# A hybrid SSD and linear-attention layer on one core: the linear-attention state in two buffers, the first sums of A beside the last scan, and w2 loaded in the first unit

## The chip, the cores and the metric

The kernel runs on one core of a Trainium2 chip. A core has a TensorE (PE: matmuls, with a part that loads weights, PEld), a VectorE (DVE), a ScalarE (ACT), a GpSimd (POOL) and a SyncE (SP, which here only issues DMAs). Each engine takes its own instructions in order, and they wait for one another by semaphores. Matmul results land in PSUM, eight banks of 512 float32 for each of 128 partitions; everything else lies in SBUF.

The metric is the device time of one execution in microseconds. A profiled execution also has a span, from its first to its last instruction.

## The reference

One layer on 2048 tokens of width 1024 with 16 meta tokens ahead of them. One input projection feeds two branches, each is projected back, weighed by sigmoid gates and merged:

```python
u = rmsnorm(hres, norm_w)
proj = jnp.einsum('bld,dn->bln', u, w_in)
z, xbc, dt_raw, q, k, v, g_gla, a_lr, merge_g = split_cols(proj, IN_WIDTHS)
...
y_r, _ = ssd_chunked(xs[:, m:], dt[:, m:], a, bm[:, m:], cm[:, m:], SSD_CHUNK, s_m)
...
o_r, _ = gla_chunked(q[:, m:], k[:, m:], v[:, m:], log_a[:, m:], GLA_CHUNK, st_m)
...
branches = jnp.stack([y_ssd.astype(y_gla.dtype), y_gla], axis=2)
branch_proj = jnp.einsum('blnc,ncd->blnd', branches, w_branch)
gates = jax.nn.sigmoid(merge_g.reshape(b, l, N_BRANCH, D_MODEL))
merged = jnp.sum(gates * branch_proj, axis=2)
return hres + jnp.einsum('bld,de->ble', merged, w_out)
```

The final RMSNorm follows, and the meta tokens are dropped. Linear attention (GLA) carries a state from chunk to chunk, for each head 128 by 256:

```python
def step(s, inp):
    qi, ki, vi, gi = inp
    o_inter = jnp.einsum('bhtk,bhkv->bhtv', qi * jnp.exp(gi), s)
    ...
    s_new = jnp.exp(g_last)[..., None] * s + jnp.einsum('bhsk,bhsv->bhkv', k_dec, vi)
    return s_new, o_inter + o_intra
```

## The kernel before

**Two halves.** The first half walks over four blocks of 512 tokens (`b`), and in each over eight units: four groups of SSD heads (`ssd_proj`, L450), then four heads of linear attention (`gla_proj`, L604). A unit projects what its heads need. It yields after each piece of projection (six times), and at each yield the loop at L830 calls `step()`, which lets every generator that has begun run on to its own next yield. So the scan of one unit (`ssd_scan` L494, `gla_scan` L639) runs beside the projection of the next ones. `gates(o)` (L414) and `dt_chain` run in the same way. The second half (from L870) is a list of products of 128 by 128 by 512 blocks: for each stage (merge gates, the two branch projections, twice, then the output projection) seven products of a Strassen-Winograd scheme for each pair of row blocks. A product needs operand tiles of B (`load_b`, `prep_b`) and of A (`load_a`, `sum_a`, `prep_a`); every one is split into a high and a low part, and three matmuls make one exact product (`accum`, L183).

**What sets the order.** On PE and SP the order is the one in which the code issues, written out by hand (`manual_schedule`). On ACT, DVE and POOL a planner places the instructions by its own estimate of times; it may bring a later one forward when its inputs are ready. A tile comes from a pool under a tag with a number of buffers; a new tile of the tag waits until one of them is free. In the second half SP too keeps its written order, and `todo` says after which product an operand is loaded, summed and split: B 12 products ahead, A's loads 9 ahead (`LOAD`), A's splits five ahead (`AHEAD`).

**w2.** `late_constants` (L332) issues four DMAs on SP: three into a staging tile for the gate weights w2, of the tag "acc" (two buffers, used by the convolution of `ssd_proj`), and one for the masks into a "tok4" tile. It is called ahead of unit 1 of block 0 (L835). Weights of the projections pass over the same SP queue (`load_w` L157, `load_raw` L173; three raw buffers), are split by ACT (L165) and POOL (L166), and are written back for the later blocks (L181).

**The meta tokens.** In block 0 `ssd_scan` first makes the state of the 16 meta tokens (`meta_state`, L515: a matmul on PE and a copy on DVE, L519), in the same step as the first chunk's matmul on that state (L565).

**The linear-attention state.** `gla_scan` ends with four chunks, two to a step (L783 to L795). The matmuls of a chunk go into the two halves of one PSUM bank `po`: kd·v into columns 256 to 511, att·v and then q·state into columns 0 to 255. Then DVE updates the state in place (L789) and ACT reads columns 0 to 255 (L791, L793).

**From the first half to the second.** When the last unit's projection is done, the scans of the last heads still run. The dictionary `between` (L1094) gives what is put ahead of each of their remaining steps `k`: the loads of B and A for products 1 and 2 of pairs 0 and 1 of the first stage, their splits and these four products. Pools opened at L860 to L862 lie where the inputs and weights lay; those opened at L1114 and L1115 lie where the scans' tiles lay, so their tiles wait for the scans. The sums of A (`sum_a`, L902, four POOL operations) of pairs 0 and 1 are made in the first `run(-1)` (L1118), from the pool `spl` of the second kind; B's raw tiles, and the snapshots of two early products (L930), come from `rpl`, of the first kind, with five buffers.

Of the kernel before, what the change touches and what calls it, by code (L numbers as in the profile page):

```python
# [20 lines left out]
SG = 4  # L21
# [19 lines left out]
def trunk_kernel(ctx: ExitStack, tc: tile.TileContext, xm, xmt, w_feat, w_tok, w_zm, w_br, w_o,  # L41
# [7 lines left out]
    def mk(pool, shape, dt, tag, **kw):  # L49
        cnt[0] += 1  # L50
        return pool.tile(shape, dt, tag=tag, name=f"{tag}_{cnt[0]}", **kw)
# [278 lines left out]
    msk = const.tile([P, NMSK, P], U8, name="msk")  # L330

    def late_constants():  # L332
        w2r = mk(wk, [P, META + BLK], F32, "acc")[:48, :512]
        for i in range(3):
            nc.sync.dma_start(w2r[16 * i:16 * i + 16, :], gw2)
        nc.scalar.activation(w2, w2r, AF.Copy)
        nc.vector.tensor_tensor(w2[32:48], w2r[32:48], w2[32:48].bitcast(F32), op=ALU.subtract)
        mstg = mk(wk, [P, D], F32, "tok4", bufs=NT4)[:, :NMSK * P]
        nc.sync.dma_start(mstg, cmsk)
        nc.vector.tensor_copy(msk.rearrange("p l t -> p (l t)"), mstg)  # L340
# [153 lines left out]
    def ssd_scan(o, g, feats, zs):  # L494
# [87 lines left out]
        yield  # L582
        if m0:
            meta_state()
        for c in range(1, NCH):
            before(c)
            after(c - 1)
            yield
# [50 lines left out]
    def gla_scan(o, h, qs, kf, vt, vm, gs):  # L639
# [140 lines left out]

        ot = mk(wk, [P, NCH, 256], F32, "ot", bufs=1)
        ssq = mk(sm, [P, 4], F32, "ssq")
        for c in range(NCH):  # L783
            po = bank(pc, "pc")
            vc = [t[:, c] for t in vt]
            accum(po[:, 256:], [t[:, c] for t in kdt], vc, True, True)
            accum(po[:, :256], [t[:, c] for t in atp], vc, True, False)
            nc.tensor.matmul(po[:, :256], qg[:, c * P:(c + 1) * P], s_gla[:, h], start=False, stop=True)
            nc.vector.scalar_tensor_tensor(s_gla[:, h], s_gla[:, h], egl[:, c:c + 1], po[:, 256:],  # L789
                                           op0=ALU.mult, op1=ALU.add)  # L790
            nc.scalar.activation(ot[:, c], po[:, :256], AF.Copy)  # L791
            jk = mk(wk, [P, 256], BF16, "junk", bufs=1)
            nc.scalar.activation(jk, po[:, :256], AF.Square, accum_out=ssq[:, c:c + 1])  # L793
            if c % 2:
                yield  # L795
# [34 lines left out]
    for b in range(nblk):  # L830
        o = new_block(b, next_u[b])
        for i in range(SG + GH):
            if (b, i) in beside:
                begin(beside_unit(beside[b, i]))
            if (b, i) == (0, 1):  # L835
                late_constants()
            if i == 1:
                begin(gates(o))
            if i == SG and b + 1 < nblk:
                begin(fetch_u(b + 1))  # L840
            for _ in ssd_proj(o, i) if i < SG else gla_proj(o, i - SG):
                step()
        save(0)


# [13 lines left out]

    bpl = {p: pool2(f"bops{p}", 4) for p in (1, 2)}  # L860
    rpl = pool2("raws", 1)
    apl = pool2("aops", 7)  # L862
    

    g_left = [[left(f"g_{b}_{i}") for i in range(16)] for b in range(nblk)]
# [4 lines left out]
    class Stage:  # L870
# [8 lines left out]
        def load_b(self, p, j):  # L879
            src = {1: lambda j: self.braw(j, 0), 2: lambda j: self.braw(4 + j, 0), 3: lambda j: self.braw(4 + j, 1),  # L880
                   4: lambda j: self.sums[1][j][:, 1], 5: lambda j: self.sums[0][j][:, 1],
                   6: lambda j: self.sums[1][j][:, 0], 7: lambda j: self.sums[0][j][:, 0]}[p]
            raw = self.braws[p, j] = mk(rpl, [P, BLK], F32, "br", bufs=5)
            nc.sync.dma_start(raw, src(j))

        def prep_b(self, p, j):
# [14 lines left out]

        def sum_a(self, n):  # L902
            a11, a21, a22, a12 = self.araws.pop(n)
            s1, s2, s4 = [mk(spl, [P, 4, P], F32, "as", bufs=6) for _ in range(3)]
            nc.gpsimd.tensor_tensor(s1, a21, a22, op=ALU.add)  # L905
            nc.gpsimd.tensor_tensor(s2, s1, a11, op=ALU.subtract)
            nc.gpsimd.tensor_tensor(a21, a11, a21, op=ALU.subtract)
            nc.gpsimd.tensor_tensor(s4, a12, s2, op=ALU.subtract)
            self.a[n].update({3: s4, 4: a22, 5: s1, 6: s2, 7: a21})
# [8 lines left out]
        def product(self, n, p, early=False):  # L918
            key, pool, tag = {1: ("a", pj, "pj"), 6: ("a",) * 3, 5: ("a",) * 3, 3: ("a",) * 3, 2: ("c", pc, "pc"),
                              7: ("b", pt, "pt"), 4: ("b",) * 3}[p]  # L920
            if p in (1, 2, 7):
                self.ps[n, key] = bank(pool, tag)
            ps = self.ps[n, key]
            a = self.a[n][p]
            for j in range(4):
                bt = self.b[p, j]
                accum(ps, (a[:, 0, j], a[:, 1, j]), (bt[:, 0], bt[:, 1]), p in (1, 2, 7) and j == 0, j == 3,
                      skip_group_check=True)
            if p in (1, 6, 5):
                sn = mk(rpl, [P, BLK], F32, "br", bufs=5) if early else mk(opl, [P, BLK], F32, "sn", bufs=6)  # L930
                nc.scalar.activation(sn, ps, AF.Copy)  # L931
                self.snap[n, p] = sn
            if p in DONE:
                key, sn = {2: ("c", 1), 5: ("b", 5), 4: ("b", 6), 3: ("a", None)}[p]
                self.use(n, *DONE[p], self.ps[n, key], self.snap.get((n, sn)))
# [57 lines left out]
    def out_stage():  # L993
        fns, res, ssq = [], {}, {}

        def fetch(n, i, t):
            r0 = (2 * n + i) * P
            r = res[n, i, t] = io()
            nc.sync.dma_start(r, xm[META + r0:META + r0 + P, t * BLK:(t + 1) * BLK])
            if t and len(fns) < 2:  # L1000
                for hf in range(2):
                    fns.append(mk(rpl, [P, BLK], F32, "br", bufs=5))
                    nc.sync.dma_start(fns[hf], fnw[:, hf * BLK:(hf + 1) * BLK].to_broadcast([P, BLK]))

        def use(n, i, t, ps, snap):
            r0 = (2 * n + i) * P
            r = res[n, i, t]
            x = total(ps, snap)
            nc.vector.scalar_tensor_tensor(r, x, 0.5, r, op0=ALU.mult, op1=ALU.add)
            first = (n, i) not in ssq  # L1010
            if first:
                ssq[n, i] = mk(spl, [P, 2], F32, "ssf")
            q = ssq[n, i]
            jk = mk(spl, [P, BLK], BF16, "junk", bufs=1)
            nc.scalar.activation(jk, r, AF.Square, accum_out=q[:, t:t + 1])
            if not first:
                nc.vector.tensor_tensor(q[:, 0:1], q[:, 0:1], q[:, 1:2], op=ALU.add)
                nc.vector.tensor_scalar(q[:, 0:1], q[:, 0:1], 1.0 / D, EPS, op0=ALU.mult, op1=ALU.add)
                nc.gpsimd.tensor_tensor(q[:, 0:1], q[:, 0:1], mhalf[:, 0:1], op=ALU.pow)
                for hf in range(2):  # L1020
                    o = res[n, i, hf]
                    nc.vector.scalar_tensor_tensor(o, o, q[:, 0:1], fns[hf], op0=ALU.mult, op1=ALU.mult)
                    store(out[r0:r0 + P, hf * BLK:(hf + 1) * BLK], o)

        return Stage("out", ("o",), seq // (2 * P),
                     lambda n, i, j: m_left[(2 * n + i) // 4][j][:, :, (2 * n + i) % 4 * P:((2 * n + i) % 4 + 1) * P],
                     fetch, use)
# [27 lines left out]
        st.sum_a(n)  # L1055

    for i, (st, n, p) in enumerate(order):
        if p == 1:
            at(i - LOAD + (n % 2), lambda st=st, n=n, i=i: st.sum_a(n) if i < NEARLY else load_sum_a(st, n))
    for si, st in enumerate(stages):  # L1060
        for q in range(0 if si else 8, 28):
            p, j = PS[q // 4], q % 4
# [25 lines left out]
    def flush(due):  # L1088
# [2 lines left out]


    st = stages[0]
    between = {  # L1094
        0: [lambda: [st.load_b(1, j) for j in range(4)], lambda: st.load_a(0)],
        1: [lambda: [st.prep_b(1, j) for j in range(4)], lambda: st.prep_a(0, 1)],
        2: [lambda: [st.load_b(2, j) for j in range(4)], lambda: st.load_a(1)],
        3: [lambda: st.product(0, 1, True), lambda: [st.prep_b(2, j) for j in range(4)], lambda: st.prep_a(0, 2)],
        4: [lambda: st.prep_a(1, 1)],
        5: [lambda: st.product(0, 2), lambda: st.prep_a(1, 2)],  # L1100
        6: [lambda: flush(stores[:]), lambda: stores.clear(), lambda: st.product(1, 1, True)],
        7: [lambda: st.product(1, 2)],
        8: [lambda: flush(stores[:]), lambda: stores.clear()],
    }
    k = 0
    while running or begun or k in between:
# [6 lines left out]
    first.close()  # L1113
    bpl.update({p: pool2(f"bops{p}", 4, side="right") for p in (6, 7, 5, 3, 4)})  # L1114
    opl, spl = pool2("outs", 1, side="right"), pool2("small", 4, side="right")  # L1115

    with tc.manual_schedule(engines={mybir.EngineType.SP}):
        run(-1)  # L1118
# [94 lines left out]
```

## Time and profile before

| | us |
|---|---|
| median of 3 runs | 2356.83 |
| lowest and highest | 2351.35, 2357.54 |
| the profiled execution's own time | 2356.45 |
| its span | 2354.7 |
| mean granted clock of TensorE | 0.985 |

| engine | busy us | share of the span |
|---|---|---|
| PE | 2252.8 | 96% |
| DVE | 1553.0 | 66% |
| ACT | 1183.3 | 50% |
| POOL | 679.4 | 29% |

The first half takes about 1560 us of the span, the second the rest. In lines of the timeline the first number is the start in microseconds from the span's beginning, the second the duration; then follow engine, source line, operation, tile written and tiles read, shape, and in brackets how long the engine was idle before it and who ended that. `SPq` and `ACTq` are DMA issues on those queues; `x4` means four instructions in a row. In lines of waits stand the total, the count and the longest one. A busy PE isn't PE at its peak: after an idle stretch the granted clock can fall to half for some microseconds.

### The profile page before, as it was taken

The page shows a single profiled execution, that of the slowest core. Times are in us where ns is not written, and L with a number is a line of the kernel's source. Part 1 is how long each engine was busy: PE and PEld are TensorE (multiplying, and loading weights), DVE is VectorE, ACT ScalarE, POOL GpSimd, SP SyncE. Part 2 cuts the span into 40 slices and gives each one's busy share as a digit, 9 for nine tenths or more (in the row PEclk, how much of TensorE's full clock was granted, in tenths as well). Part 3 has the DMA queues.
Part 4 walks back from the last instruction along what each step waited for, and adds up shares of the span by engine and source line. Part 5 has one row for each costly group of instructions (what it writes and reads, how often), then busy time and mean ns, then how long its engine had stood idle before and what let it go on. Part 6 is the DMA issues. An engine that isn't in the chain of part 4 may idle for free.

```text
span 2354.7 us, 36479 instructions
## 1 busy us (share of the span) xinstructions
PE 2252.8 (96%) x12641; PEld 1956.3 (83%) x12641; DVE 1553.0 (66%) x2895; ACT 1183.3 (50%) x2758; POOL 679.4 (29%) x681
## 2 busy tenths in 40 slices
PE   7799999999999999999999999879999999999998
PEld 7689889889888988888988898758888878878786
DVE  5577665666576667566568655664578864778875
ACT  4565655455534455543456443554554444554543
POOL 3334433122311212221122200037423254413341
PEclk9899999999999999999999999989999999999999
DMA  7665875666886666787676655547577866777753
GB/s 270 216 209 180 301 243 186 207 218 212 265 269 201 209 220 215 241 259 225 194 227 217 206 169 161 171 146 237 193 236 269 293 230 202 256 259 255 254 165 116
DMA packets 301545, 518.05 MB, mean 220 GB/s; under 512 B 27696, under 2 KB 143664, under 8 KB 301360
## 3 DMA queue, kind: packets, MB, share of 16 engines
q1 hardware_dynamic: 200400, 402.84, 53.0%
q10 hardware_dynamic: 100960, 112.88, 13.9%
q8 instruction: 99, 1.62, 0.3%
q14 instruction: 86, 0.70, 0.1%
HBM read 368.42 MB, written 147.19 MB: 219 GB/s over the span
## 4 chain that ended last, share of the span: by engine, by line
PE 36%; DMA 6%; DVE 4%; issue 3%; ACT 2%; SPq 1%; POOL 0%; ACTq 0%; DVEq 0%; POOLq 0%
PE pj L187 8%; PE pj L185 8%; PE pj L186 8%; PE pt L187 2%; PE pt L185 2%; PE pt L186 2%; DMA br<-br_t 2%; DVE b L890 1%; PE pc L186 1%; PE pc L187 1%; PE pc L185 1%; DMA m<-io 1%; DVE a L915 1%; DMA br<-gate_t 1%; PE pc L698 1%
## 5 line engine op out<-in xcount | busy, mean ns | idle before, releaser
L185 PE MATMUL pj<-u,whl 128*128 128x512 f32 (+1 forms) x1184 | 447.2, 378 | 11.7 <-ACT g_all L437 3.6
L187 PE MATMUL pj<-u,whl 128*128 128x512 f32 (+1 forms) x1184 | 431.2, 364 | 0.8 <-POOL whl L166 0.8
L186 PE MATMUL pj<-u,whl 128*128 128x512 f32 (+1 forms) x1184 | 429.9, 363 | 0.0
L185 PE MATMUL pj<-whl,u 128*128 128x256 f32 (+1 forms) x992 | 290.8, 293 | 8.4 <-ACT whl L165 6.9
L187 PE MATMUL pj<-whl,u 128*128 128x256 f32 (+1 forms) x992 | 284.0, 286 | 1.5 <-DVE u L300 1.5
L186 PE MATMUL pj<-whl,u 128*128 128x256 f32 (+1 forms) x992 | 284.1, 286 | 1.1 <-POOL whl L166 1.1
L185 PEld LDWEIGHTS pj<-u,whl 128*128 128x128 f32 x1184 | 225.4, 190 | 49.7 <-ACT g_all L437 4.0
L185 PE MATMUL pj<-b,a 128*128 128x512 f32 x640 | 253.1, 399 | 11.5 <-ACT sn L931 6.8
L187 PE MATMUL pj<-b,a 128*128 128x512 f32 x640 | 252.9, 395 | 5.9 <-DVE a L915 5.9
L187 PEld LDWEIGHTS pj<-u,whl 128*128 128x128 f32 x1184 | 224.7, 190 | 36.8 <-POOL whl L166 1.1
L186 PEld LDWEIGHTS pj<-u,whl 128*128 128x128 f32 x1184 | 225.4, 190 | 33.5
L186 PE MATMUL pj<-b,a 128*128 128x512 f32 x640 | 251.6, 393 | 0.0
L185 PEld LDWEIGHTS pj<-whl,u 128*128 128x128 f32 x992 | 191.7, 193 | 9.6 <-ACT whl L165 7.1
L890 DVE TENSOR_TENSOR b<-br,b 128x512 fp32r<-128x512 f32 x196 | 160.0, 839 | 51.5 <-ACT b L889 51.2
L186 PEld LDWEIGHTS pj<-whl,u 128*128 128x128 f32 x992 | 191.7, 193 | 2.1 <-POOL whl L166 1.7
L187 PEld LDWEIGHTS pj<-whl,u 128*128 128x128 f32 x992 | 191.5, 193 | 2.2 <-DVE u L300 2.2
L80 POOL TENSOR_TENSOR wr<-wr 128x256 f32<-128x256 f32 x80 | 67.5, 843 | 428.3 <-DMA wr<-y 173.2
L166 POOL TENSOR_TENSOR whl<-wr,whl 128x512 fp32r<-128x512 f32 (+1 forms) x100 | 131.7, 1323 | 188.5 <-ACT whl L165 154.8
L889 ACT ACTIVATE b<-br 128x512 fp32r<-128x512 f32 x196 | 119.3, 627 | 112.9 <-DMA br<-br_t 43.4
L905 POOL TENSOR_TENSOR as<-ar,ar 128x512 f32<-128x512 f32 x40 | 56.4, 1410 | 414.7 <-DMA ar<-in_w_br 174.8
L915 DVE TENSOR_TENSOR a<-ar,a 128x512 fp32r<-128x512 f32 x160 | 131.3, 835 | 65.3 <-ACT a L914 62.2
L479 DVE SCALAR_TENSOR_TENSOR acc<-cin,hcw,acc 128x512 f32<-128x512 f32 (+1 forms) x192 | 154.5, 805 | 27.1 <-ACT acc L475 26.6
(274 smaller groups left out, 5057.3 us busy)
## 6 DMA issues: line engine op xcount, KB each, us to landing
whl<-k_s SPq DMA_DIRECT2D x96, 512.0 KB, 4.5
whl<-k_g SPq DMA_DIRECT2D x96, 512.0 KB, 4.1
whl<-k_v SPq DMA_DIRECT2D x48, 512.0 KB, 3.8
whl<-k_z SPq DMA_DIRECT2D x36, 512.0 KB, 3.7
wr<-in_w_feat SPq DMA_DIRECT2D x64, 256.0 KB, 4.4
k_s<-whl SPq DMA_DIRECT2D x32, 512.0 KB, 3.6
cb<-cumd ACTq DMA_DIRECT2D x64, 256.0 KB, 5.3
y<-gg ACTq DMA_DIRECT2D x64, 256.0 KB, 4.5
```

What stands on the lines that cost most here:

```text
L80: nc.gpsimd.tensor_tensor(o, x, y, op=ALU.subtract)
L166: nc.gpsimd.tensor_tensor(hl[:, 1], raw, hl[:, 0].bitcast(F32), op=ALU.subtract)
L185: nc.tensor.matmul(ps, sh, mh, start=first, stop=False, **kw)
L186: nc.tensor.matmul(ps, sh, ml, start=False, stop=False, **kw)
L187: nc.tensor.matmul(ps, sl, mh, start=False, stop=last, **kw)
L479: nc.vector.scalar_tensor_tensor(acc, cin[:, k:k + tt], hcw[:, ti, k:k + 1], acc, op0=ALU.mult, op1=ALU.add)
L698: nc.tensor.matmul(ps[:, r * P:(r + 1) * P], kq[:, 2 * r * P:(2 * r + 1) * P], kq[:, (2 * r + 1) * P:(2 * r + 2) * P], start=True, stop=True)
L889: nc.scalar.activation(t[:, 0], raw, AF.Copy)
L890: nc.vector.tensor_tensor(t[:, 1], raw, t[:, 0].bitcast(F32), op=ALU.subtract)
L905: nc.gpsimd.tensor_tensor(s1, a21, a22, op=ALU.add)
L915: nc.vector.tensor_tensor(t[:, 1], src, t[:, 0].bitcast(F32), op=ALU.subtract)
```

## The change

The update of the linear-attention state moves ahead of att·v, and the state alternates between its old place and a new tile "st". `late_constants` is called in the first unit after its second step, and w2's staging tile comes from the tag "act" (eight buffers). `ssd_scan` yields once more in block 0, after `meta_state`. Between the halves B's raw tiles of products 1 and 2 come from a ring of two ("br0") and are loaded and split two at a time; the later ones come from five "br" buffers of the pool `opl`. The sums of A for pairs 0 and 1 are made at k = 6 and k = 8, in tiles of `rpl`, which also hold the two early snapshots. The pool of A's operands has six buffers in place of seven.

```diff
     def late_constants():
-        w2r = mk(wk, [P, META + BLK], F32, "acc")[:48, :512]
+        w2r = mk(wk, [P, META + BLK], F32, "act", bufs=NACT)[:48, :512]
...
         if m0:
             meta_state()
+            yield
         for c in range(1, NCH):
...
+        states = [s_gla[:, h], mk(wk, [P, 256], F32, "st", bufs=1)]
         for c in range(NCH):
             po = bank(pc, "pc")
             vc = [t[:, c] for t in vt]
+            old, new = states[c % 2], states[1 - c % 2]
             accum(po[:, 256:], [t[:, c] for t in kdt], vc, True, True)
+            nc.vector.scalar_tensor_tensor(new, old, egl[:, c:c + 1], po[:, 256:], op0=ALU.mult, op1=ALU.add)
             accum(po[:, :256], [t[:, c] for t in atp], vc, True, False)
-            nc.tensor.matmul(po[:, :256], qg[:, c * P:(c + 1) * P], s_gla[:, h], start=False, stop=True)
-            nc.vector.scalar_tensor_tensor(s_gla[:, h], s_gla[:, h], egl[:, c:c + 1], po[:, 256:],
-                                           op0=ALU.mult, op1=ALU.add)
+            nc.tensor.matmul(po[:, :256], qg[:, c * P:(c + 1) * P], old, start=False, stop=True)
...
-            if (b, i) == (0, 1):
-                late_constants()
...
-            for _ in ssd_proj(o, i) if i < SG else gla_proj(o, i - SG):
+            for n, _ in enumerate(ssd_proj(o, i) if i < SG else gla_proj(o, i - SG)):
                 step()
+                if (b, i, n) == (0, 0, 1):
+                    late_constants()
...
-    apl = pool2("aops", 7)
+    apl = pool2("aops", 6)
+    bt_raws = {"early": (rpl, "br0", 2)}
...
-            raw = self.braws[p, j] = mk(rpl, [P, BLK], F32, "br", bufs=5)
+            pool, tag, nb = bt_raws.get("all") or bt_raws["early"]
+            raw = self.braws[p, j] = mk(pool, [P, BLK], F32, tag, bufs=nb)
...
-            s1, s2, s4 = [mk(spl, [P, 4, P], F32, "as", bufs=6) for _ in range(3)]
+            s1, s2, s4 = [mk(rpl, [P, 4, P], F32, "as", bufs=6) for _ in range(3)]
...
-                sn = mk(rpl, [P, BLK], F32, "br", bufs=5) if early else mk(opl, [P, BLK], F32, "sn", bufs=6)
+                sn = mk(rpl, [P, 4, P], F32, "as", bufs=6).rearrange("p k c -> p (k c)") if early else mk(opl, [P, BLK], F32, "sn", bufs=6)
...
-        if p == 1:
-            at(i - LOAD + (n % 2), lambda st=st, n=n, i=i: st.sum_a(n) if i < NEARLY else load_sum_a(st, n))
+        if p == 1 and i >= NEARLY:
+            at(i - LOAD + (n % 2), lambda st=st, n=n: load_sum_a(st, n))
...
+    def b_ops(p, js):
+        for j in js:
+            st.load_b(p, j)
+            st.prep_b(p, j)
...
-        0: [lambda: [st.load_b(1, j) for j in range(4)], lambda: st.load_a(0)],
-        1: [lambda: [st.prep_b(1, j) for j in range(4)], lambda: st.prep_a(0, 1)],
-        2: [lambda: [st.load_b(2, j) for j in range(4)], lambda: st.load_a(1)],
-        3: [lambda: st.product(0, 1, True), lambda: [st.prep_b(2, j) for j in range(4)], lambda: st.prep_a(0, 2)],
+        0: [lambda: st.load_a(0), lambda: b_ops(1, (0, 1))],
+        1: [lambda: b_ops(1, (2, 3)), lambda: st.prep_a(0, 1)],
+        2: [lambda: st.load_a(1), lambda: b_ops(2, (0, 1))],
+        3: [lambda: st.product(0, 1, True), lambda: b_ops(2, (2, 3)), lambda: st.prep_a(0, 2)],
...
-        6: [lambda: flush(stores[:]), lambda: stores.clear(), lambda: st.product(1, 1, True)],
+        6: [lambda: flush(stores[:]), lambda: stores.clear(), lambda: st.product(1, 1, True), lambda: st.sum_a(0)],
         7: [lambda: st.product(1, 2)],
-        8: [lambda: flush(stores[:]), lambda: stores.clear()],
+        8: [lambda: flush(stores[:]), lambda: stores.clear(), lambda: st.sum_a(1)],
...
+    bt_raws["all"] = opl, "br", 5
```

More of the change, by code (lines that the diff above doesn't have):

```diff
@@ L1001, in fetch @@
                 for hf in range(2):
-                    fns.append(mk(rpl, [P, BLK], F32, "br", bufs=5))
+                    fns.append(mk(opl, [P, BLK], F32, "br", bufs=5))
                     nc.sync.dma_start(fns[hf], fnw[:, hf * BLK:(hf + 1) * BLK].to_broadcast([P, BLK]))
```

## The prediction

> **What bounds the kernel now.** I read the page first, then the PE's waits, then the timeline around each wait that the diff touches.
>
> ```profile
> span 2354.7 us, 36479 instructions
> PE 2252.8 (96%) x12641; PEld 1956.3 (83%) x12641; DVE 1553.0 (66%) x2895; ACT 1183.3 (50%) x2758; POOL 679.4 (29%) x681
> ```
>
> PE is busy for 2252.8 of 2354.7 us, so the whole of its idle time is 101.9 us. Whatever the change gains it takes from there (and from stretches in which PE's granted clock was halved after an idle stretch); whatever new wait it puts into PE's order is added almost in full, because PE takes its instructions in the order written by hand and has no slack in which to make it up. The waits of PE, by who ended them (us in total, times, longest):
>
> ```profile
> PE pj L185 <- ACT whl L165: 10.2, 2, 6.9
> ...
> PE pc L788 <- DVE s_gla L789: 9.2, 7, 2.9
> ```
>
> Two parts of the diff touch these two (weights that come late, the state of linear attention); the two others touch single waits of 4 to 5 us, shown below.
>
> **The state of linear attention.** Before, a chunk issues on PE three matmuls kd·v into columns 256 to 511 of bank po, three att·v into columns 0 to 255, then q·state; after these DVE updates the state from columns 256 to 511. After the change DVE's update stands between kd·v and att·v. It reads the bank that att·v writes next, other columns of it. Whether att·v must then wait is the main question. Nothing in this trace has PE write a bank of which DVE has just read another part. The nearest rows are of DVE and ACT, from the views of L789 (the engine that ended the idle time before it, then who waited for it) and of L436:
>
> ```profile
>   PE pc L788: 70.4, 37
> who waited for it (us, times):
>   ACT ot L791: 19.0, 25
> ```
> ```profile
> who waited for it (us, times):
>   ACT g_all L437: 7.4, 6
> ```
>
> L791 reads columns 0 to 255 and needs nothing of L789, which reads columns 256 to 511; yet it waited for it 25 times, 19.0 us. L437 and L436 read the same bank and write different tiles, and L437 waited 6 times. So this program keeps two engines out of one bank in the order in which they are written down, reads against reads included. I take it that a PE write is held behind a DVE read in the same way.
>
> The Trainium skill ("PSUM — Partial Sum Buffer", section "PSUM bank collisions raise a hardware error") says that no two of TensorE, ScalarE and VectorE may use one bank at once, whichever columns, and that semaphores are to guard it by bank. By that rule att·v waits and the sum is the one below; by columns it would be the first rival's. No run here shows yet a PE write that is held so.
>
> The price of the wait, from one chunk (start, duration), one late update, and one start of PE after a wait:
>
> ```profile
> 723.09 0.28 PE L187 MATMUL pc<-tok,kdt 128*128 128x256 f32 x1
> 723.21 0.28 PE L185 MATMUL pc<-tok,atp 128*128 128x256 f32 x1
> ...
> 723.57 0.59 PE L788 MATMUL pc<-s_gla,act 128*128 128x256 f32 x2
> ```
> ```profile
> 724.20 0.48 DVE L789 SCALAR_TENSOR_TENSOR s_gla<-s_gla,egl,pc 128x256 f32<-128x256 f32 x1 [5.72 <-PE pc L788]
> ```
> ```profile
> 342.54 0.47 DVE L789 SCALAR_TENSOR_TENSOR s_gla<-s_gla,egl,pc 128x256 f32<-128x256 f32 x1
> ```
> ```profile
> 343.07 1.14 PE L788 MATMUL pc<-s_gla,act 128*128 128x256 f32 x2 [2.12 <-DVE s_gla L789]
> ```
> ```profile
> 42.79 0.39 PE L185 MATMUL pj<-u,whl 128*128 128x264 f32 x1 [0.77 <-ACT acc L475]
> 43.02 0.28 PE L186 MATMUL pj<-u,whl 128*128 128x264 f32 x1
> ```
>
> A free DVE starts 0.04 us after the matmul that it waits for (724.16 to 724.20), so after the third kd·v (end 723.37) it would start at 723.41 and end at 723.89; PE goes on 0.06 us after DVE's end (343.01 to 343.07), at 723.95 where it stood at 723.21: 0.74 us. The first matmul after a wait holds the next one 0.23 us (42.79 to 43.02) instead of the 0.12 above: 0.11 us more. That is 0.85 us a chunk; 64 chunks (4 heads, 4 blocks, 4 chunks): 54.4 us. Behind the held att·v stand q·state, the next chunk and the next projection; no other engine has the work to cover it.
>
> That is with DVE free. In 37 of 64 updates DVE waited for PE; in 27 it was still busy. The first and the last of these:
>
> ```profile
> 339.65 0.59 PE L788 MATMUL pc<-s_gla,act 128*128 128x256 f32 x2
> ...
> 1523.11 0.70 PE L788 MATMUL pc<-s_gla,act 128*128 128x256 f32 x2
> ```
> ```profile
> 1525.79 0.47 DVE L789 SCALAR_TENSOR_TENSOR s_gla<-s_gla,egl,pc 128x256 f32<-128x256 f32 x1
> ```
>
> They are 2.3 us (340.24 to 342.54) and 2.0 us late; all 27, read off the timeline in the same way, add up to 24.9 us. The order on DVE is made by a planner, which will place the update earlier, and a PE that waits lets DVE catch up; I take half, 12.4 us. The old wait of PE for the update, 9.2 us, goes, since the new state is ready before att·v even starts. Together **54.4 + 12.4 - 9.2 = +57.6 us**. Ends: no lateness, +45; DVE's present order kept, every update behind the work that it follows now, counted from the third kd·v: 98 us in place of 47 (64 x 0.74), so +96. Without any wait: -9.2.
>
> **w2 in the first unit.** SP's queue, in order, before unit 1, then PE, then two stretches (busy time of the engines; the third number from the end is PE's granted clock, the last one GB/s):
>
> ```profile
> 43.75 0.42 SPq L175 DMA_DIRECT2D wr<-in_w_feat  x1
> 60.48 1.25 SPq L335 DMA_DIRECT2D acc<-in_gw  x3
> 61.77 0.42 SPq L339 DMA_DIRECT2D tok<-in_cmsk  x1
> ```
> ```profile
> 68.44 0.58 PE L185 MATMUL pj<-whl,u 128*128 128x256 f32 x1 [6.86 <-ACT whl L165]
> 69.84 0.58 PE L186 MATMUL pj<-whl,u 128*128 128x256 f32 x1 [0.82 <-POOL whl L166]
> ```
> ```profile
> 68.00:74.00 6.00, 4.47 (x19) 3.88 (x20) 0.00 (x0) 1.65 (x3) 3.81 (x3) 0.54 1.00 351
> 104.00:108.00 4.00, 3.80 (x14) 3.44 (x15) 3.77 (x10) 1.82 (x5) 0.79 (x1) 0.54 0.28 97
> ```
>
> SP stands from 44.2 to 60.5 us before L335, whose tile is one of two "acc" buffers that the convolution still uses; the weights of unit 1 are queued behind it and PE idles 6.86 + 0.82 us, then runs 4.47 us at a clock of 0.54 (4.47 x 0.46 = 2.1 us lost). With a free "act" tile this goes: -9.8. But the four DMAs now pass in front of the first feature weights of unit 0:
>
> ```profile
> 33.11 1.29 POOL L166 TENSOR_TENSOR whl<-wr,whl 128x512 fp32r<-128x512 f32 x1 [3.48 <-ACT whl L165]
> ```
> ```profile
> 34.65 0.37 PE L185 MATMUL pj<-u,whl 128*128 128x264 f32 x1
> ```
>
> These weights are ready 0.25 us before PE takes them, and the four issues take 1.25 + 0.42 us on SP, so PE is 1.4 us late there; the mask is 0.46 MB, at the 351 GB/s of the stretch above 1.3 us more. I take 2.2: **-7.6 us** (ends -9.8 and -4). The ACT copy and two DVE operations only change place.
>
> **The yield after the meta state.**
>
> ```profile
> 103.75 0.39 DVE L519 COPY s_ssd<-pc 128x256 f32<-128x256 f32 x1
> ```
> ```profile
> 104.20 0.79 PE L565 MATMUL pc<-s_ssd,act 128*128 128x256 f32 x1 [4.77 <-DVE s_ssd L519]
> ```
>
> L565 of the first head group comes right behind the matmul whose copy DVE reaches late. With a projection step between (48 matmuls at 0.12 us, 5.8 us), 4.77 us go, and the halved clock after it (3.80 x 0.46 = 1.7): **-6.5 us** (ends -9 and 0, if DVE's scans hold up the copy's neighbours in the new place). The four scans of block 0 end a step later, under the next unit's projection.
>
> **The end of the scans.**
>
> ```profile
> 1563.49 0.80 PE L185 MATMUL pj<-b,a 128*128 128x512 f32 x1 [4.55 <-ACT a L914]
> 1564.08 0.63 PE L186 MATMUL pj<-b,a 128*128 128x512 f32 x1
> 1569.18 0.80 PE L187 MATMUL pj<-b,a 128*128 128x512 f32 x1 [4.48 <-DVE a L915]
> ```
> ```profile
> 1560.87 7.66 DVE L890 TENSOR_TENSOR b<-br,b 128x512 fp32r<-128x512 f32 x5 [1.14 <-ACT b L889]
> 1568.45 0.68 DVE L915 TENSOR_TENSOR a<-as,a 128x512 fp32r<-128x512 f32 x1
> ```
> ```profile
> 1561.18 1.75 POOL L905 TENSOR_TENSOR as<-ar,ar 128x512 f32<-128x512 f32 x1
> ```
>
> Five L890 take 7.66 us there, where five of the 0.68 us of the next row would take 3.4: POOL makes the sums of A in the same stretch (its row last, one of eight). Made beside the last scan, they leave 4.3 us to DVE. Against it: B's raws for product 6 now lie in the space of the scans and are loaded later than before, and the ring of two makes SP wait for L890 between pairs of loads, with the A tiles of pair 1 queued behind it. I take **-5 us** (ends: both waits and the slow clock, -11; loads late by a few us, +3). Six "a" buffers for seven: operands are still made five products ahead; nothing taken, end +4.
>
> **Sum**: 57.6 - 7.6 - 6.5 - 5 = +38.5 us. The profiled execution's own time is 2356.45 us (1.75 outside the span), 0.4 below the median of 2356.83. Forecast **2395 us**.
>
> **Rivals.** (1) The other side: att·v is not held, because DVE reads other columns. Then the new order costs nothing: -9.2 - 7.6 - 6.5 - 5 = -28.3, 2328 us. For it: no element is shared. Against: 31 waits of L791 and L437. It decides at some 0.3 us of wait a chunk: 64 x 0.3 = 19.1 us eat up all the other gains. (2) The hold is there and DVE's order stays: 96 - 19.1 = +77, 2433 us. For: the updates up to 2.3 us late; against: those are the pairs of chunks where another head starts, and the planner sees the wait. (3) The other edits don't do what they say: the weights' gap moves to unit 0, B's raws come as late as the sums did, together -3 instead of -19.1: +54.6, 2411 us. For: 0.25 us of slack.
>
> **Chances.** Forecast 0.65, rivals 0.15, 0.10 and 0.10. The range 2364 to 2434 takes in the forecast with the ends of its terms, rivals 2 and 3, and leaves out rival 1. Within 0.3% (about what a measurement here can tell from no change) lie 2349 to 2364, the forecast's lowest tail: 0.05. Faster 0.15, slower 0.80.
>
> **What would show it.** Right: the waits of PE list att·v (L185, tile pc) behind DVE's update 64 times with at least 0.6 us each, and L788 no longer waits for it; SP has no stop near 44 us; L565 has no wait at 104 us; L890 after the scans takes 0.68 us. Wrong: att·v following kd·v by 0.12 us as now.

## The result, and the profile after

| | before | after |
|---|---|---|
| median of 6 runs (us) | 2356.97 | 2410.77 |
| lowest and highest | 2351.35, 2360.41 | 2404.93, 2413.88 |
| profiled execution | 2356.45 | 2413.88 |

The ratio is 1.0226, with a 95% interval of 1.0208 to 1.0244: 53.8 us slower by the medians, where 38.5 were forecast.

The page of the kernel after (busy time and share of the span):

```profile
span 2412.1 us, 36628 instructions
...
PE 2274.3 (94%) x12641; PEld 1973.1 (82%) x12641; DVE 1567.9 (65%) x2895; ACT 1187.4 (49%) x2758; POOL 681.6 (28%) x681
```

Of the 57.4 us by which the span grew, PE's idle time makes 35.9 (137.8 against 101.9) and its busy time 21.5: the same 12641 matmuls also took longer. Both have to be explained.

The waits of PE after (who waited, on which line, for whom: us in total, times, longest). L185 is `accum`'s first matmul, L790 the update, L795 ACT's read of columns 0 to 255:

```profile
PE pc L185 <- DVE st L790: 38.5, 31, 4.5
PE pc L185 <- DVE s_gla L790: 19.5, 28, 1.6
...
PE pc L185 <- ACT junk L795: 5.0, 4, 1.8
...
PE pc L185 <- ACT atp L233: 0.7, 1, 0.7
```

So all 64 first matmuls of att·v wait, 63.7 us in all. For 59 the profile names the update. For four it names L795 and for one ACT's split of att (L233), each of which ended at most 0.12 us after the update of that chunk: these too stand behind it. Updates into "st" are those of a head's first and third chunk, those into "s_gla" of its second and fourth; the four of L795 are second chunks, the one of L233 is a first. Four such waits of one head, from the timeline of PE after:

```profile
326.28 0.55 PE L185 MATMUL pc<-tok,atp 128*128 128x256 f32 x1 [3.34 <-DVE st L790]
329.42 0.55 PE L185 MATMUL pc<-tok,atp 128*128 128x256 f32 x1 [0.66 <-DVE s_gla L790]
339.79 0.38 PE L185 MATMUL pc<-tok,atp 128*128 128x256 f32 x1 [0.57 <-DVE st L790]
341.77 0.39 PE L185 MATMUL pc<-tok,atp 128*128 128x256 f32 x1 [0.57 <-DVE s_gla L790]
```

0.57 us is the wait with DVE free; it is also the shortest of all. The first wait is six times that long. From the stretches of the kernel after (busy PE, PEld, DVE, ACT and POOL; then PE's granted clock; then DMA), what DVE and the clock did there:

```profile
320.00:324.00 4.00, 2.94 (x15) 2.25 (x13) 4.00 (x9) 1.51 (x4) 1.40 (x1) 1.00 0.81 261
324.00:328.00 4.00, 1.72 (x6) 1.57 (x7) 2.66 (x7) 3.96 (x12) 0.58 (x1) 0.61 0.61 189
328.00:332.00 4.00, 3.34 (x14) 2.89 (x13) 1.08 (x2) 1.46 (x6) 0.69 (x1) 0.50 0.55 196
332.00:336.00 4.00, 4.00 (x23) 4.00 (x23) 0.00 (x0) 0.04 (x1) 0.00 (x0) 0.61 0.02 5
```

DVE is full for 4.00 of 4.00 us while PE already stands: the update sits behind older work of DVE. Then the clock is halved for some 10 us (0.39 of 4 us means 3.1 us at half speed, then 4, then 3.1), in which PE has work for 9.06 us and loses up to 3.9 of them (1.72 x 0.39 + 3.34 x 0.50 + 4.00 x 0.39). A stall so costs a second time.

The Trainium skill ("TensorE: Matmul & The Clock Gate", section "What's actually happening") says that the clock falls to half after an idle window of some 3.4 us and comes back after a busy one. Here the fall came earlier and the return later: PE's last matmul before the stop ended at 322.94, and 3.1 us at half speed before 328 begin at 324.9, some 2 us into the stop; full speed came back some 9 us after PE had started again at 326.28, with a wait of 0.66 us in between.

### The profile page after: what moved, and what is told of

Same layout as the page of the kernel before. It is cut to its first block, busy times and chain, and to the rows that moved or that the text cites. A ratio compares the mean times of both kernels' runs of the same rounds, so it can differ in the third digit from the quotient of the medians.

```text
span 2412.1 us, 36628 instructions
## 1 busy us (share of the span) xinstructions
PE 2274.3 (94%) x12641; PEld 1973.1 (82%) x12641; DVE 1567.9 (65%) x2895; ACT 1187.4 (49%) x2758; POOL 681.6 (28%) x681
## 3 DMA queue, kind: packets, MB, share of 16 engines
q1 hardware_dynamic: 200400, 402.84, 50.8%
## 5 line engine op out<-in xcount | busy, mean ns | idle before, releaser
L185 PE MATMUL pj<-u,whl 128*128 128x512 f32 (+1 forms) x1184 | 451.6, 381 | 16.6 <-ACT acc L475 6.4
L185 PE MATMUL pj<-whl,u 128*128 128x256 f32 (+1 forms) x992 | 290.0, 292 | 1.5 <-ACT u L298 1.5
L185 PEld LDWEIGHTS pj<-u,whl 128*128 128x128 f32 x1184 | 228.6, 193 | 56.4 <-ACT acc L475 7.5
L185 PE MATMUL pj<-b,a 128*128 128x512 f32 x640 | 255.3, 399 | 10.8 <-ACT sn L935 6.9
L187 PEld LDWEIGHTS pj<-u,whl 128*128 128x128 f32 x1184 | 227.5, 192 | 38.3 <-POOL whl L166 2.1
L186 PEld LDWEIGHTS pj<-u,whl 128*128 128x128 f32 x1184 | 228.4, 193 | 34.0
L185 PEld LDWEIGHTS pj<-whl,u 128*128 128x128 f32 x992 | 190.8, 192 | 2.9 <-ACT u L298 2.0
L894 DVE TENSOR_TENSOR b<-br,b 128x512 fp32r<-128x512 f32 x196 | 154.2, 807 | 48.1 <-ACT b L893 47.3
```

Source lines behind the costliest of these rows:

```text
L185: nc.tensor.matmul(ps, sh, mh, start=first, stop=False, **kw)
L186: nc.tensor.matmul(ps, sh, ml, start=False, stop=False, **kw)
L187: nc.tensor.matmul(ps, sl, mh, start=False, stop=last, **kw)
L894: nc.vector.tensor_tensor(t[:, 1], raw, t[:, 0].bitcast(F32), op=ALU.subtract)
```

## Experiments on the state

**gla_only**: the kernel before with this part alone (the changed lines of `gla_scan`, as in the diff above).

> The kernel before with the linear-attention part of the change alone (update between kd.v and att.v, two state buffers). Theory of the bank (att.v is held behind DVE's read of the same bank): about 58 us above before, 2415, with some 60 waits of att.v for the update of at least 0.57 us each. Rival theory (the loss comes from the other edits, the moved loads and pools): within 10 us of before.

Measured: 2430.3 us, 1.0325 of before [1.028, 1.0369], some 75 us more. (Each experiment's ratio is to runs of the kernel before that were made with it; their medians are 2353.7 to 2355.4 us.) Its waits of PE:

```profile
PE pc L185 <- DVE st L789: 39.2, 31, 4.1
PE pc L185 <- DVE s_gla L789: 18.8, 28, 1.3
```

They are those of the kernel after. The part costs more than the whole change, so the other parts gain.

**no_gla**: the kernel after with this part undone, so the other parts alone.

```diff
-        states = [s_gla[:, h], mk(wk, [P, 256], F32, "st", bufs=1)]
...
-            nc.vector.scalar_tensor_tensor(new, old, egl[:, c:c + 1], po[:, 256:], op0=ALU.mult, op1=ALU.add)
             accum(po[:, :256], [t[:, c] for t in atp], vc, True, False)
-            nc.tensor.matmul(po[:, :256], qg[:, c * P:(c + 1) * P], old, start=False, stop=True)
+            nc.tensor.matmul(po[:, :256], qg[:, c * P:(c + 1) * P], s_gla[:, h], start=False, stop=True)
+            nc.vector.scalar_tensor_tensor(s_gla[:, h], s_gla[:, h], egl[:, c:c + 1], po[:, 256:],
+                                           op0=ALU.mult, op1=ALU.add)
```

> The changed kernel with the linear-attention part undone. Theory of the bank: the other edits gain some 10 to 20 us, 2337 to 2347, and PE waits for the update about 9 us again, at q.state. Rival (the other edits cost): near 2400.

Measured: 2335.2 us, 0.9919 of before [0.9895, 0.9943]. The page:

```profile
span 2334.6 us, 36513 instructions
...
PE 2250.2 (96%) x12641; PEld 1955.2 (84%) x12641; DVE 1553.2 (67%) x2895; ACT 1184.5 (51%) x2758; POOL 686.6 (29%) x681
```

Against the kernel after, 77.5 us of span: 53.4 of PE's idle time (137.8 less 84.4) and 24.1 of its busy time. The same head in the stretches of no_gla has a wait too, but the clock stays full:

```profile
320.00:324.00 4.00, 2.47 (x17) 2.12 (x15) 3.83 (x9) 1.89 (x7) 1.39 (x1) 1.00 0.83 283
324.00:328.00 4.00, 3.23 (x25) 3.18 (x26) 2.42 (x5) 3.81 (x14) 1.77 (x1) 1.00 0.28 68
328.00:332.00 4.00, 4.00 (x35) 4.00 (x34) 0.00 (x0) 1.69 (x4) 1.29 (x1) 1.00 0.77 269
```

And over the whole span (the view of the cores, after and then no_gla):

```profile
core 0: 2412.1 us, clock 0.976
```
```profile
core 0: 2334.6 us, clock 0.986
```

Taking half as the only other speed, 0.976 means 116 us at half clock (2 x 0.024 x 2412) and 0.986 means 65: the waits bring some 50 us more of it. (By the medians over all runs, 0.978 and 0.986, it is some 40.) PE has work in 85 us of this time after and in 47 us in no_gla, by the clock records of the two traces; half of the difference, 19 us, is what the clock costs of the 24.1 us of busy time.

**own_bank** keeps the early update and the two buffers, and gives kd·v a bank of its own. If the bank is what holds att·v, the waits go; if an early update is itself too much for DVE, they stay.

```diff
-            accum(po[:, 256:], [t[:, c] for t in kdt], vc, True, True)
-            nc.vector.scalar_tensor_tensor(new, old, egl[:, c:c + 1], po[:, 256:], op0=ALU.mult, op1=ALU.add)
+            pk = bank(pt, "pt")
+            accum(pk[:, :256], [t[:, c] for t in kdt], vc, True, True)
+            nc.vector.scalar_tensor_tensor(new, old, egl[:, c:c + 1], pk[:, :256], op0=ALU.mult, op1=ALU.add)
```

> The changed kernel with kd.v written to a bank of its own (of the transposes' three), so that the update reads no bank that att.v writes; update still early, two state buffers. Theory of the bank: no wait of att.v for the update, 2335 to 2348, at most a few us from the kernel without the part. Rival theory (it is DVE's late update itself that PE waits for, whichever bank): the waits move to q.state and the time stays above 2395.

Measured: 2331.97 us, 0.9909 of before [0.9873, 0.9944]. Of the update, only q·state (L793) still waits:

```profile
PE pc L793 <- DVE st L791: 10.6, 7, 3.0
```

No att·v waits for the update: an early update alone does not hold att·v, it does so only through the shared bank. By the median, 79 us went with it. A tile is a whole bank here, so this run can't tell a guard by bank from one by tile.

**late_update** keeps the two buffers and puts the update behind q·state, where it was.

```diff
-            nc.vector.scalar_tensor_tensor(new, old, egl[:, c:c + 1], po[:, 256:], op0=ALU.mult, op1=ALU.add)
             accum(po[:, :256], [t[:, c] for t in atp], vc, True, False)
             nc.tensor.matmul(po[:, :256], qg[:, c * P:(c + 1) * P], old, start=False, stop=True)
+            nc.vector.scalar_tensor_tensor(new, old, egl[:, c:c + 1], po[:, 256:], op0=ALU.mult, op1=ALU.add)
```

> The changed kernel with two state buffers, but the update behind q.state as before, in the same bank. Theory of the bank: no hold, within 5 us of the kernel without the linear-attention part (2337 to 2347), so the second buffer by itself is worth nothing. Rival (the second buffer, its alternation or its space costs): above 2360.

Measured: 2337.04 us, 0.9931 [0.9905, 0.9956]. The second buffer by itself is worth nothing that can be told from no_gla's 0.9919. The bank is shared here too, so it takes both, the shared bank and the early update. Without the hold these three kernels lie between 2332 and 2337 us; the hold costs 74 to 79 us by the medians, and 70 to 75 by the ratios.

**hold_first and hold_second** give only half of the chunks the shared bank: the first and third of a head, or the second and fourth (`c % 2 == 0`, then `== 1`).

```diff
-            accum(po[:, 256:], [t[:, c] for t in kdt], vc, True, True)
-            nc.vector.scalar_tensor_tensor(new, old, egl[:, c:c + 1], po[:, 256:], op0=ALU.mult, op1=ALU.add)
+            pk = po[:, 256:] if c % 2 == 0 else bank(pt, "pt")[:, :256]
+            accum(pk, [t[:, c] for t in kdt], vc, True, True)
+            nc.vector.scalar_tensor_tensor(new, old, egl[:, c:c + 1], pk, op0=ALU.mult, op1=ALU.add)
```

> The kernel after, with kd v of the second and fourth chunk of each head in a bank of its own, so that only the 32 updates of the first and third chunk can hold att v. Without any hold this kernel took 2332 to 2337, with all 64 2411, 75.6 us more. If each hold costs the same: half of it, some 2372. If a hold costs in proportion to how late DVE is (waits of 38.5 + 5.0 us of the 63.0 stand behind the updates of the first and third chunk): 0.69 of 75.6 = 52, some 2386. If DVE, with fewer holds to follow, catches up: 64 x 0.58 / 2 = 19 us of waits and no more than 2360.

> The same the other way round: only the 32 updates of the second and fourth chunk can hold att v. Equal price: some 2372. In proportion to the lateness (19.5 us of the 63.0): 0.31 of 75.6 = 23, some 2357. By the plain length of the update alone (waits of 0.58 us, as for a free DVE): 19 us of waits, 2353.

Measured: hold_first 2370.49 us, 1.0058 [1.004, 1.0077]; hold_second 2361.1 us, 1.0029 [1.0015, 1.0044]. The pages and the waits of PE, hold_first's and then hold_second's:

```profile
span 2370.2 us, 36581 instructions
...
PE 2259.0 (95%) x12641; PEld 1963.2 (83%) x12641; DVE 1562.2 (66%) x2895; ACT 1187.8 (50%) x2758; POOL 684.8 (29%) x681
```
```profile
PE pc L185 <- DVE st L791: 30.5, 31, 3.9
...
PE pc L185 <- ACT atp L233: 0.7, 1, 0.7
```
```profile
span 2355.4 us, 36579 instructions
...
PE 2249.2 (95%) x12641; PEld 1955.6 (83%) x12641; DVE 1551.8 (66%) x2895; ACT 1184.9 (50%) x2758; POOL 685.9 (29%) x681
```
```profile
PE pc L185 <- DVE s_gla L791: 27.6, 30, 3.5
...
PE pc L185 <- ACT act L661: 3.3, 1, 3.3
...
PE pc L185 <- ACT sq L688: 2.2, 1, 2.2
```

In each all 32 att·v in the shared bank wait (the ACT lines are att·v whose update ended at most 0.15 us ahead of what is named).

The expectations put the 5.0 us of L795 with the first and third chunks; they belong to the second. So in the kernel after the first and third chunks have 39.2 us of the waits and the others 24.5, and the theory of lateness expects 2382 and 2364 in place of 2386 and 2357.

Over no_gla's 2335.2 the two cost 35 and 26 us. The first fits an equal price for each hold (2372), the second is nearer to the lateness (2364), so neither theory fits both. The waits speak for the equal price: 31.2 and 33.1 us, together 64.3 where the kernel after has 63.7. The third theory, that DVE catches up, expected 19 us in each and falls. When only the second chunk of a pair is held, it pays (longest 3.5 us, average 1.03) for work of DVE that the first had waited for before (there the second's longest was 1.8, the average 0.77). So the lateness goes with the place in DVE's queue, not with the chunk.

The two costs sum to 61, the whole hold to 75.6. Idle time nearly sums (26.8 + 21.8 against no_gla, 53.4 for the whole) and the busy time does not (+8.8 and -1.0, against +24.1). By these single profiles it is the growth of busy time, the slow clock in the main, that comes only when there are many waits. The median granted clocks over all runs point the same way (0.983 and 0.985, against 0.986 for no_gla and 0.978 for the whole). That it is their nearness is argued, not shown, and the difference of 14 us is not much above what the intervals leave open.

## Experiments on the other parts

**w2_only**: the kernel before with w2 loaded in the first unit (the staging tile, and the call after the second step of unit 0).

> The kernel before with the w2 part alone. The prediction's term: -7.6 us, so some 2349 (0.9968 of before). In the trace: no stop of 6.9 us near 68 us; the first feature weights of unit 0 come 1.4 to 2.5 us late at 35 us. Rival: the late start at 35 us lets the clock fall there as it did at 68, and the gain is below 3 us (2354 or more).

Measured: 2343.55 us, 0.9957 [0.9941, 0.9972]. Its timeline of PE, with one later matmul, and the same matmul in the kernel before:

```profile
36.19 0.39 PE L185 MATMUL pj<-u,whl 128*128 128x264 f32 x1 [1.61 <-ACT whl L165]
46.17 0.59 PE L185 MATMUL pj<-u,whl 128*128 128x264 f32 x1 [1.53 <-ACT acc L475]
295.01 0.45 PE L185 MATMUL pj<-whl,u 128*128 128x256 f32 x1
```
```profile
302.43 0.56 PE L185 MATMUL pj<-whl,u 128*128 128x256 f32 x1
```

The stop of 6.86 us at 68 us is gone, 1.61 us of it is back at unit 0's weights, and by 300 us the kernel is 7.4 us ahead. The term of -7.6 lies in the interval (-13.9 to -6.6 us). The rival's slow clock does not come at 35 us: the granted clock is 1.00 from 32 to 44 us.

**yield_only**: the kernel before with the one added `yield`.

> The kernel before with the yield after the meta state alone. The prediction's term: -6.5 us, so some 2350 (0.9972). In the trace: no wait of L565 for the copy L519 at 104 us. Rival, from the trace after the change: ACT's work of the scan bunches a step later and a projection waits 4.4 us for ACT near 145 us, so the gain is some 0 to -2 us (2355 or more).

Measured: 2343.64 us, 0.9955 [0.9941, 0.9969]. Two matmuls of its timeline of PE, and the first of them in the kernel before:

```profile
99.12 0.39 PE L185 MATMUL pj<-u,whl 128*128 128x264 f32 x1
155.25 0.59 PE L185 MATMUL pj<-u,whl 128*128 128x264 f32 x1 [4.20 <-ACT acc L475]
```
```profile
105.71 0.78 PE L185 MATMUL pj<-u,whl 128*128 128x264 f32 x1
```

Right behind the old wait it is 6.6 us ahead. Two things in that figure nearly cancel: 15 matmuls of the scan are still to come there, and the profile stood 1.1 us behind ahead of the wait. Where both kernels have made the same number of matmuls (112.72 and 107.53 us) the lead is 5.2 us, so 6.3 us were won, and the predicted term is 6.5. The rival's new wait of 4.20 us for ACT is there as well. That the whole run still gains 10.6 us (7.3 to 13.9) is more than these two together. The lead grows and shrinks later in the first half at no one place, and why it ends higher was not settled.

**between_only**: the kernel before with the rest of the change, the end of the scans and the six "a" buffers.

> The kernel before with the sums of A beside the last scan, B's raws in rings, and six buffers for A's operands. The prediction's term: -5 us, so some 2352 (0.998). The comparison of the traces of before and after says more: some 13 us gained in the second half, so 2344 (0.9945). Rival: five products ahead with one buffer fewer makes splits wait, and it is 2357 or more. The three parts are to sum to the -20 us of the kernel with the state's part undone; where they sum to less than 15, the parts help one another.

Measured: 2350.85 us, 0.9984 [0.9973, 0.9996]: 3.8 us (0.9 to 6.4), and not the 13 that the comparison of the traces of before and after had suggested. The end of the scans in the kernel after, from the timelines of PE, ACT, DVE and SP (`x4`: four instructions):

```profile
1629.20 1.22 PE L185 MATMUL pj<-b,a 128*128 128x512 f32 x2 [3.89 <-ACT b L893]
```
```profile
1628.52 0.63 ACT L893 ACTIVATE b<-br 128x512 fp32r<-128x512 f32 x1 [4.59 <-DMA br<-gate_t]
```
```profile
1632.18 2.58 DVE L894 TENSOR_TENSOR b<-br,b 128x512 fp32r<-128x512 f32 x4 [0.76 <-ACT b L893]
```
```profile
1625.34 10.90 SPq L888 DMA_DIRECT2D br<-gate_t  x12
```

Without POOL's sums beside it, DVE's subtractions of B take 0.65 us each (2.58 / 4) in place of 1.53 (7.66 / 5), and the second of the two waits is gone. (POOL has no work from 1622.2 to 1652.0 us.) But B's raws are asked for only at 1625.34, and PE waits 3.89 us for the first of them: one wait is replaced by another.

The three parts alone come to -10.1, -10.6 and -3.8 by their ratios, -24.5; together, in no_gla, to -19.1 (-24.7 to -13.4). Within the intervals they add up.

## A version that beats both

**early_kv** takes the idea further: kd·v and the update of chunk c+1 go behind q·state of chunk c, in a bank of their own, so that DVE has a whole chunk's time. w2 comes two steps later.

```diff
+        def update(c):
+            pk = bank(pt, "pt")
+            accum(pk[:, :256], [t[:, c] for t in kdt], [t[:, c] for t in vt], True, True)
+            nc.vector.scalar_tensor_tensor(states[1 - c % 2], states[c % 2], egl[:, c:c + 1], pk[:, :256],
+                                           op0=ALU.mult, op1=ALU.add)
+
+        update(0)
...
-            accum(po[:, 256:], [t[:, c] for t in kdt], vc, True, True)
-            nc.vector.scalar_tensor_tensor(new, old, egl[:, c:c + 1], po[:, 256:], op0=ALU.mult, op1=ALU.add)
...
-            nc.tensor.matmul(po[:, :256], qg[:, c * P:(c + 1) * P], old, start=False, stop=True)
+            nc.tensor.matmul(po[:, :256], qg[:, c * P:(c + 1) * P], states[c % 2], start=False, stop=True)
+            if c + 1 < NCH:
+                update(c + 1)
...
-                if (b, i, n) == (0, 0, 1):
+                if (b, i, n) == (0, 0, 3):
```

> The kernel after, with kd v in a bank of its own and issued with its update one chunk ahead, behind the q state matmul of the chunk before; and w2 loaded two steps later in unit 0. If the bank is what cost the time, and a state that is early is worth the waits of 3.7 to 10.6 us left in the three kernels without the hold: 2322 to 2332 (0.985 to 0.9895). The first feature weights of unit 0 no longer come late (1.6 us in the trace after). Rival: a second pt bank for each chunk makes the next scores or decays wait for a free bank, and it is 2337 or more.

**early_kv_w2 and early_kv_w2b** differ only in the place of w2: `(0, 0, 1)` as in the change, and `(0, 0, 2)`.

> The kernel early_kv with w2 loaded where the change loads it (after the second step of unit 0). early_kv had one stop of 10.7 us at 58 us, behind w2; here that stop is to be gone and the one of 1.6 us at 36 us back: 9 us and some of the slow clock behind it, 2316 to 2320 (0.984 of before). Rival: the stop at 58 us only moves, and it is 2325 or more.

> The same with w2 one step later (after the third step of unit 0). If the first feature weights pass ahead of w2 here and the weights of unit 1 aren't held up either, neither stop is left: 2313 to 2318. Rival: the stop of 10.7 us is already here: 2326 or more.

Measured: early_kv 2327.67 us, 0.9887 [0.9871, 0.9902]; early_kv_w2 2317.3 us, 0.984 [0.9816, 0.9863]; early_kv_w2b 2326.41 us, 0.9888 [0.9861, 0.9915]. The one wait of PE that w2 leaves in each, in that order:

```profile
58.59 0.59 PE L185 MATMUL pj<-u,whl 128*128 128x264 f32 x1 [10.72 <-ACT whl L165]
```
```profile
35.49 0.39 PE L185 MATMUL pj<-u,whl 128*128 128x264 f32 x1 [1.60 <-ACT whl L165]
```
```profile
47.41 0.59 PE L185 MATMUL pj<-u,whl 128*128 128x264 f32 x1 [5.69 <-ACT whl L165]
```

10.72, 1.60 and 5.69 us behind weights: the place that the change chose is the best of the three. The hope of a place without any wait fell. Why the later places cost more isn't shown: in early_kv SP stands from 38.3 to 50.8 us right behind the four loads, but what it waited for its trace doesn't show clearly. Nor do the stops explain all of the times: w2b stops 4 us longer than w2 and takes 9 us more. Both stay open. early_kv came into its range with a stop that was not foreseen.

In early_kv_w2 no matmul waits for an update any more, and its 64 updates (grouped by form; last, DVE's idle time before them, and on whom it waited) are waited for by nobody:

```profile
L785 DVE SCALAR_TENSOR_TENSOR s_gla<-st,egl,pt 128x256 f32<-128x256 f32 x32 | 15.3, 478 | 48.2 <-PE pt L187 48.2
L785 DVE SCALAR_TENSOR_TENSOR st<-s_gla,egl,pt 128x256 f32<-128x256 f32 x32 | 15.2, 477 | 9.7 <-PE pt L187 9.6
```

DVE waits for PE now (57.9 us of idle time), and that costs nothing. This version is 36 us faster than the kernel before and 93 us faster than the one after. Part of it is the bank alone (own_bank 0.9909); the chunk of lead brings it to 0.984.

## Why the prediction was right, and where it was short

- **att·v is held**: right. All 64 wait; the shortest, 0.57 us, is the idle time that its working has between 723.37 and 723.95. "At least 0.6" was a hair too high. Rival 1, no hold because the columns differ, fell: the waits are there, and own_bank, which changes nothing but the bank, takes them away. The Trainium skill's rule ("PSUM — Partial Sum Buffer", section "PSUM bank collisions raise a hardware error") is borne out as far as this program goes: the program's semaphores keep two engines out of one bank, whichever columns. What two engines would do in one bank without them, no run tried. As foretold, q·state (now L792) no longer waits for the update.
- **The size of the hold**: mis-sized. +57.6 was predicted; 70 to 79 us are measured. The step that failed is "I take half, 12.4 us": of the 63.7 us of waits, 64 x 0.57 = 36.5 are the free wait and 27.2 lateness, as much as the 24.9 that the trace of before had shown. A waiting PE did not let DVE catch up. This alone (14.8 us) would nearly close the gap, but two more misses partly cancel, by luck. The term had nothing for the clock, which took some 19 us of PE's time. And of its 0.85 us a chunk, 0.27 is not waiting but matmuls that no longer overlap, 17 us in 64 chunks; in the profiles only some 5 us of busy time are left for that (24.1 less 19). Rival 2 named the lateness but counted it for every update (96), too much again.
- **w2, -7.6**: right, with the measured gain (6.6 to 13.9) at or above it, and right in its two parts. The wait of 1.61 us is the "1.4 us late" of the step, and SP's queue in the kernel after has no stop left where it stood from 44.2 to 60.5 us:

```profile
44.85 0.42 SPq L175 DMA_DIRECT2D wr<-in_w_feat  x1
46.66 0.33 SPq L181 DMA_DIRECT2D k_s<-whl  x1
47.04 0.42 SPq L175 DMA_DIRECT2D wr<-in_w_feat  x1
48.74 0.33 SPq L181 DMA_DIRECT2D k_s<-whl  x1
```

- **The yield, -6.5**: right at its place (6.3 us); the run as a whole gained more, 7.3 to 13.9, for a reason not found.
- **The end of the scans, -5**: right (0.9 to 6.4), with one of the two waits replaced by late raws, which the term named as its risk. L894 takes 0.65 to 0.69 us, as foretold.
- **The sum**: the other terms were predicted at -19.1 and measured together at -19.1 (-24.7 to -13.4, so the match to the decimal is luck), and the missing 15 us lie in the hold (53.8 + 19.1 = 72.9 by these, 57.6 predicted). Rival 3 has the time that was measured, 2411, but by accident: it needed the other terms to shrink to -3, and they did not. The forecast of 2395 for 2410.77 us had the sign, the mechanism and the other three terms.

## What to carry to other kernels

Before an update moves ahead of a matmul, look in which PSUM bank the matmul writes. In this program the update read other columns of that bank, and the matmul still waited for the whole of it and for whatever the other engine had queued ahead of it. A new wait of a saturated PE is to be priced with the lateness that the old trace shows at that very place, in full, and with the slow clock that may follow. The cure here was a bank of its own and one chunk of lead; in these runs neither cost time.

## What was not expected of the hardware

The clock: one stop of 3.34 us brought some 10 us at half speed, and the kernel's 63.7 us of waits some 50 us more of half clock, while half as many waits (hold_second, 33.1 us) brought no longer busy time at all in its profile. How near to one another waits must be for that, these runs do not tell.
